# Pooled rows kept whole in HBM and split where they are fetched, in a hybrid encoder block on one Trainium2 core

## The chip, the cores and the metric

One core of one Trainium2 chip runs the whole kernel. The metric is the device time of one execution in microseconds (us). A core has five engines with a queue of instructions each: TensorE (PE, matrix products), VectorE (DVE), ScalarE (ACT), GpSimd (POOL) and SyncE (SP, which here only issues transfers). An engine works its queue in order: an instruction that waits holds everything behind it on the same engine. Transfers (DMAs) are issued here from SP's and from ACT's queue.

## The reference

One layer (`DEPTH = 1`) of a bidirectional hybrid encoder on x (1 x 1024 x 1024, float32):

```python
h = rmsnorm(x, norm_mix)
q, k, v, r, lr_f, lr_b, u, g_a, g_b = split(h @ w_in)
y_a = swish-gated, normed gated linear attention, forward plus backward, @ w_branch_gla
y_b = per group: (multiscale_pool(u)[g] @ w_pool_group[g]) * pool_scale
x = x + (sigmoid(g_a) * y_a + sigmoid(g_b) * y_b) @ w_out
x = x + swiglu(rmsnorm(x, norm_ffn) @ w_ffn_in) @ w_ffn_out
```

and a final RMSNorm. What matters here is branch B. `u` has 512 channels in four groups of 128; for group g, `multiscale_pool` takes a centred mean over 2, 4, 8 or 16 positions (only valid ones at the ends) and subtracts the token itself:

```python
window_sum = cs[:, hi, gi] - cs[:, lo, gi]
return window_sum / count - ug
```

Each pooled group (128 channels x 1024 positions) is then multiplied by a 128 x 256 matrix and by the gate `sigmoid(g_b)`.

## The kernel before

**Arithmetic.** Every matrix product is made in full precision from reduced-precision parts (`fp32r`). An operand is split into a high part, cast by ACT, and a low part, the difference, made by DVE or POOL; three matmuls (hi x hi, lo x hi, hi x lo) are added up in PSUM (`products`, L288-L291, so nearly all matmuls have the line L291). The large projections go through a seven-product scheme: of two 2 x 2 blocked operands, seven products of sums of blocks are formed in place of eight. One product of this kind is 12 matmuls of 128x512.

**Stages.** Norm and projections of q, k, v; the two scans of the attention; then the *gate stage* (L1316-L1361); then the branch products, the merge with `w_out`, the feed-forward layer and the last norm. The gate stage makes the columns of `w_in` for the pool input and the gates in ten units of 256 columns, n = 0 to 9: units 0 and 1 are the pool input `u`, 2 to 5 gate A, 6 to 9 gate B. Run n of the loop over `gate_runs` has seven products, in the order 1, 5, (product 4 of unit n-1), 6, 2, 3, 7; the last run also does its own product 4 at the end. `at` counts the products in a run. In `Gates.run`, the results of products 1, 6 and 5 are copied by ACT to the row `ga` (L1281), those of 2, 3 and 7 added to it by DVE (L1286), and a sigmoid follows on ACT (L1289). Banks of PSUM are shared: 1, 6, 7 and 4 of a unit accumulate in one, 5 and 3 in another, so product 6 waits until the copy of product 1 is done, product 7 for the copy of 6, product 3 for that of 5, and product 4 for the add of 7. For a gate-B unit g = n - 6, after products 7 and 4, `Gates.pooling` makes the group's own product `yb` from the split pooled rows `ph`, `pl` and the split `w_pool_group` (three blocks after 7, one after 4).

**Weights.** A unit's weight halves are loaded by SP (`fraw`, L910), summed by DVE where the scheme wants a sum (`fs`, L918), cast by ACT (`wh`, L198) and their low parts made mostly by POOL (`wl`, L199).

**What sets the order.** After every three matmuls `mm3` calls `pump` with the share of a product's quarter that has passed (1 for 512 columns). `pump` runs what is due: steps put off with `soon(delay, step)`, stores that were put on a list with `later` (`pending`), one generator of jobs (`aside`) and one generator of side work (`side`). Each of these yields a cost, and the next step comes when as many units of `pump` have passed. So the numbers in the source set at which place in each engine's queue a step is written, and nothing is reordered later.

**Pooling** is the generator `pooling` (L1235), begun in run 2 at `at == 4`. For each group it loads the rows of `u`, calls `pooled` (window sums on DVE in tiles `ws`, per half of the 1024 positions), and stores the result to `p_out` in HBM. `pooled` yields after each operation and `pooling` multiplies this cost by `POOLING`. `load_pooled(g)` brings it back into two slots (`ph`, `pl`) in run 6 + g.

**Feed-forward jobs.** Two units of `w_ffn_in` (`READY = 2`) get their seven weight operands in the gate stage: `unit_jobs` loads two raw halves into slots (`fraw`, L534), POOL makes four sums in place (L637), and each of the seven operands is cast by ACT (`uph`, L629), gets its low part from DVE (`upl`, L620), and both parts are stored to HBM in `u_out` from ACT's queue (L631, L616). The parts stand in the pool `t2`, which has five buffers that pooling's `u` and `ws` also use. The jobs come through `prepare_beside(jobs, 2.7, ...)`, one step each 2.7 units of `pump`.

## Time and profile before

| What | us |
|---|---|
| three runs | 1383.60, 1383.58, 1387.52 (median 1383.6) |
| the profiled execution | 1385.57 |
| its span, first to last instruction | 1383.8 |
| PE busy | 1362.2 (98%) |
| DVE, POOL, ACT busy | 848.3, 757.6, 625.1 |
| mean granted TensorE clock | 0.999 of full speed |

Times in the traces count from the start of the span. In a row of a timeline stand the start in us, the duration in us, the engine, the line of the kernel, the operation, output and inputs by the program's names, the shape, and in brackets how long the engine was idle ahead of it and what ended that. In a table of waits stand the engine, its waiting operation, what it waited for, then us in total, how often and the longest. In a tile's view stand the durations min/median/max in ns and the first and last start in us.

### The profile page before, as it was taken

What the parts mean: (1) busy time and instruction counts of PE and PEld (TensorE: products, weight loads), DVE (VectorE), ACT (ScalarE), POOL (GpSimd) and SP (SyncE); (2) the same over time, 40 slices, a digit from 0 to 9 for tenths busy, and PEclk for the clock granted to TensorE, in tenths of its full rate; (3) what the DMA queues carried; (4) which work ended last, traced back from release to release, by engine and by line L of the source; (5) the groups of instructions that cost most, each with busy time, mean ns of one, the idle gap of its engine ahead of it and who ended that gap; (6) DMA issues with size and microseconds to landing.
All of it is one profiled execution on the core that took longest, in us unless ns stands there. A gap on an engine that the chain in (4) does not pass through costs nothing.

```text
span 1383.8 us, 18503 instructions
## 1 busy us (share of the span) xinstructions
PE 1362.2 (98%) x6654; PEld 1150.9 (83%) x6654; DVE 848.3 (61%) x1073; ACT 625.1 (45%) x1125; POOL 757.6 (55%) x565
## 2 busy tenths in 40 slices
PE   7999999999999999999999999999999999999997
PEld 7889898988888877788888788888888888888886
DVE  6276767766645885587884856555655556343374
ACT  7365655644334444554346533333333334453252
POOL 3260715312398456568665276666666667464354
PEclk9999999999999999999999999999999999999999
DMA  6221322321487669997416355555444447975451
GB/s 193 77 92 44 110 82 87 122 77 46 138 264 238 211 198 310 334 393 257 152 61 240 118 175 175 175 175 175 159 141 141 145 137 267 385 256 216 167 232 73
DMA packets 167452, 243.56 MB, mean 176 GB/s; under 512 B 10904, under 2 KB 97856, under 8 KB 167360
## 3 DMA queue, kind: packets, MB, share of 16 engines
q1 hardware_dynamic: 154368, 215.11, 46.7%
q10 hardware_dynamic: 12992, 27.27, 5.3%
q8 instruction: 52, 0.85, 0.3%
q14 instruction: 40, 0.33, 0.1%
HBM read 164.48 MB, written 77.86 MB: 175 GB/s over the span
## 4 chain that ended last, share of the span: by engine, by line
PE 81%; POOL 5%; issue 4%; DVE 4%; ACT 3%; DMA 2%; ACTq 0%; POOLq 0%; SPq 0%; DVEq 0%
PE ps L291 75%; POOL wl L199 2%; PE op L849 2%; DMA u_out<-uph 1%; PE kv L291 1%; PE sc L777 1%; PE op L291 1%; POOL qe L733 1%; DVE res L1796 1%; POOL wsum L637 1%; PE yb L291 1%; PE tp L1008 1%; DMA u_out<-upl 0%; DMA raw<-in_w_in_dram 0%; DVE ws L1068 0%
## 5 line engine op out<-in xcount | busy, mean ns | idle before, releaser
L199 POOL TENSOR_TENSOR wl<-fs,wh 128x512 fp32r<-128x512 f32 x120 | 166.2, 1389 | 163.9 <-ACT wh L198 139.4
L291 PE MATMUL ps<-gl,wh 128*128 128x512 f32 x616 | 239.8, 389 | 0.9 <-DVE gl L1488 0.9
L291 PE MATMUL ps<-gh,wh 128*128 128x512 f32 x616 | 240.4, 390 | 0.0
L291 PE MATMUL ps<-gh,wl 128*128 128x512 f32 x616 | 239.7, 389 | 0.0
L199 POOL TENSOR_TENSOR wl<-fraw,wh 128x512 fp32r<-128x512 f32 x90 | 130.1, 1445 | 64.3 <-ACT wh L198 59.5
L199 POOL TENSOR_TENSOR wl<-raw,wh 128x512 fp32r<-128x512 f32 x44 | 63.8, 1463 | 159.0 <-ACT wh L198 158.9
L199 POOL TENSOR_TENSOR ol<-gor,oh 128x1024 fp32r<-128x1024 f32 (+1 forms) x42 | 99.8, 2382 | 92.3 <-ACT oh L198 71.8
L291 PE MATMUL ps<-hh,wh 128*128 128x512 f32 x376 | 149.8, 398 | 0.0
L291 PE MATMUL ps<-hh,wl 128*128 128x512 f32 x376 | 146.6, 390 | 0.0
L291 PE MATMUL ps<-hl,wh 128*128 128x512 f32 x376 | 146.5, 390 | 0.0
L291 PEld LDWEIGHTS ps<-gl,wh 128*128 128x128 f32 x616 | 115.7, 188 | 25.1 <-DVE gl L1488 1.3
L291 PEld LDWEIGHTS ps<-gh,wl 128*128 128x128 f32 x616 | 115.6, 188 | 24.0
L291 PEld LDWEIGHTS ps<-gh,wh 128*128 128x128 f32 x616 | 115.7, 188 | 23.6
L291 PE MATMUL ps<-ol,oh 128*128 128x512 f32 x308 | 119.9, 389 | 0.2 <-DVE ol L199 0.2
L291 PE MATMUL ps<-oh,oh 128*128 128x512 f32 x308 | 119.8, 389 | 0.0
L291 PE MATMUL ps<-oh,ol 128*128 128x512 f32 x308 | 119.8, 389 | 0.0
L199 POOL TENSOR_TENSOR wl<-wraw,wh 128x512 fp32r<-128x512 f32 x56 | 91.3, 1659 | 46.0 <-ACT wh L198 46.0
L199 DVE TENSOR_TENSOR ol<-wor,oh 128x1024 fp32r<-128x1024 f32 (+1 forms) x41 | 61.4, 1520 | 49.5 <-ACT oh L198 49.3
L198 ACT CAST wh<-fs 128x512 fp32r<-128x512 f32 x120 | 73.8, 615 | 32.1 <-DVE fs L918 23.8
L291 PEld LDWEIGHTS ps<-hh,wl 128*128 128x128 f32 x376 | 70.6, 188 | 15.0
L291 PEld LDWEIGHTS ps<-hl,wh 128*128 128x128 f32 x376 | 70.7, 188 | 13.2
L291 PEld LDWEIGHTS ps<-hh,wh 128*128 128x128 f32 x376 | 70.7, 188 | 13.2
(262 smaller groups left out, 3176.4 us busy)
## 6 DMA issues: line engine op xcount, KB each, us to landing
fraw<-in_w_ffn_in_dram SPq DMA_DIRECT2D x44, 512.0 KB, 6.2
gor<-g_out SPq DMA_DIRECT2D x35, 512.0 KB, 7.1
raw<-in_w_in_dram SPq DMA_DIRECT2D x48, 256.0 KB, 3.8
g_out<-s SPq DMA_DIRECT2D x44, 256.0 KB, 2.3
fraw<-in_w_in_dram SPq DMA_DIRECT2D x20, 512.0 KB, 4.5
wor<-t_out SPq DMA_DIRECT2D x20, 512.0 KB, 7.6
g_out<-g SPq DMA_DIRECT2D x33, 256.0 KB, 2.6
x<-in_x_dram SPq DMA_DIRECT2D x16, 512.0 KB, 4.3
```

Source lines behind the costliest of these rows:

```text
L198: nc.scalar.copy(hi, src)
L199: eng.tensor_tensor(lo, src, as_f32(hi), op=ALU.subtract)
L291: nc.tensor.matmul(ps, a[i], b[j], start=first and n == 0, stop=last and n == 2, skip_group_check=onto)
L637: op()
L733: nc.gpsimd.tensor_tensor(e_q[:, d, :], e_q[:, d, :], q[:, half, :], op=ALU.mult)
L777: nc.tensor.matmul(sc[d][:, i * CH : (i + 1) * CH], chunk_of(ke, n, d), chunk_of(qe, n, d), start=True, stop=True,)
L849: nc.tensor.matmul(op[:, :DV], a, b, start=False, stop=j == len(terms) - 1)
L1008: nc.tensor.transpose(tp[:, i * P : (i + 1) * P], o_heads[j // 2][half][:, i, (j % 2) * P : (j % 2 + 1) * P], ident[:, :],)
L1796: nc.vector.scalar_tensor_tensor(res[:, COLS[j]], x2[t][:, COLS[j]], rs[:, :], gain_final[:, COLS[j]], op0=ALU.mult, op1=ALU.mult)
```

## The change

`pooled` no longer splits its result. The last operation of each half writes straight into one tile of 128 x 2 x 512 float32, and the group is stored with one transfer of 512 KB. `load_pooled` fetches it with one transfer into the slot `pl`, one product earlier than before (`at == 2` for 3). Two new steps split it on the spot: `cast_pooled` takes a second slot `ph` and casts all 1024 columns on ACT; `low_pooled` subtracts in place on DVE. They are put off by 2.5 and 4.3 units from the end of `at == 4` (in the last run of `at == 3`). `POOLING` goes from 1.75 to 2.5 and two yields around the stores go. And the two feed-forward units are begun at `at == 1` of run 6 where it was `at == 4`, three products sooner.

```diff
-POOLING = 1.75
+POOLING = 2.5
...
-    def pooled(g, u, hi, lo):
+    def pooled(g, u, raw):
...
             nc.vector.scalar_tensor_tensor(
-                s[:, body], s[:, body], 1.0 / width, u[half][:, body], op0=ALU.mult, op1=ALU.subtract
+                raw[:, half, :], s[:, body], 1.0 / width, u[half][:, body], op0=ALU.mult, op1=ALU.subtract
             )
             yield 1
-            nc.scalar.copy(hi[:, half, :], s[:, body])
-            yield 1
-            nc.vector.tensor_tensor(lo[:, half, :], s[:, body], as_f32(hi[:, half, :]), op=ALU.subtract)
-            yield 0.2
...
-    p_out = dram.tile([GROUPS, 2, P, 2, HALF], F32, name="p_out")
+    p_out = dram.tile([GROUPS, P, 2, HALF], F32, name="p_out")
...
-        pools[g] = [slot(F32R, s=s) for s in ("ph", "pl")]
-        for n, t in enumerate(pools[g]):
-            nc.sync.dma_start(as_f32(t[:, :, :]), p_out[g][n])
+        t = slot(F32R, s="pl")
+        nc.sync.dma_start(as_f32(t[:, :, :]), p_out[g])
+        pools[g] = [None, t]
+
+    def cast_pooled(g):
+        pools[g][0] = slot(F32R, s="ph")
+        nc.scalar.copy(pools[g][0][:, :, :], as_f32(pools[g][1][:, :, :]))
+
+    def low_pooled(g):
+        hi, t = (t[:, :, :] for t in pools[g])
+        nc.vector.tensor_tensor(t, as_f32(t), as_f32(hi), op=ALU.subtract)
...
-            hi, lo = slot(F32R, s="ph"), slot(F32R, s="pl")
-            for cost in pooled(g, u, hi, lo):
+            raw = slot(s="pr")
+            for cost in pooled(g, u, raw):
                 yield POOLING * cost
-            nc.scalar.dma_start(p_out[g][0], as_f32(hi[:, :, :]))
-            yield 4
-            nc.scalar.dma_start(p_out[g][1], as_f32(lo[:, :, :]))
+            nc.scalar.dma_start(p_out[g], raw[:, :, :])
             stored.add(g)
-            yield 1
+            yield 2
...
                 if n == 2:
                     begin(pooling(), 4)
-                if n == 6:
-                    finish_side()
-                    finish_beside()
-                    prepare_beside(map(unit_jobs, range(READY)), 2.7, 1, 1, nc.scalar)
+            if n == 6 and at == 1:
+                finish_side()
+                finish_beside()
+                prepare_beside(map(unit_jobs, range(READY)), 2.7, 1, 1, nc.scalar)
...
-            if n >= 6 and at == (0 if last else 3):
+            if n >= 6 and at == (0 if last else 2):
                 load_pooled(n - 6)
+            if n >= 6 and at == (3 if last else 4):
+                soon(2.5, partial(cast_pooled, n - 6))
+                soon(4.3, partial(low_pooled, n - 6))
```

PE's instructions stand in the same order in both kernels. The changed kernel's lines lie a few numbers lower or higher: L1281, L1286 and L1289 become L1283, L1288 and L1291.

*DVE, end of unit 5 (run 5).* `ga` is the row of unit 5's results (the adds of product 3 and of product 7), `ws` and `u` are pooling's window sums and rows of group 3. Before:

```order
L1286 TENSOR_TENSOR ga_4978<-ps_4984,ga_4978 128x512
L1088 TENSOR_TENSOR pl_5049<-ws_5089,ph_5048 128x512
L1068 TENSOR_TENSOR ws_5118<-u_5024 128x527
L1074 TENSOR_TENSOR ws_5126<-ws_5118 128x525
L1286 TENSOR_TENSOR ga_5000<-ps_4961,ga_5000 128x512
```

Now:

```order
L1288 TENSOR_TENSOR ga_4970<-ps_4976,ga_4970 128x512
L1074 TENSOR_TENSOR ws_5098<-ws_5079 128x521
L1074 TENSOR_TENSOR ws_5106<-ws_5098 128x513
L1288 TENSOR_TENSOR ga_4992<-ps_4950,ga_4992 128x512
```

Between the two adds the low part and the first two sums of the second half are gone, and the two last sums of that half have come.

*SP, run 7.* The transfers for group 1 of the pooled rows, for the next gate unit (`fraw`, L910) and for the second feed-forward unit (`fraw`, L534). Before:

```order
L910 DMA fraw_5354<-in_w_in_dram 128x8x128
L910 DMA fraw_5384<-in_w_in_dram 128x8x128
L1223 DMA ph_5422<-p_out 128x1024
L1223 DMA pl_5423<-p_out 128x1024
L534 DMA fraw_5481<-in_w_ffn_in_dram 128x8x128
L534 DMA fraw_5482<-in_w_ffn_in_dram 128x8x128
L1227 DMA wpr_5493<-in_w_pool_group_dram 128x256
```

Now:

```order
L910 DMA fraw_5357<-in_w_in_dram 128x8x128
L534 DMA fraw_5389<-in_w_ffn_in_dram 128x8x128
L534 DMA fraw_5390<-in_w_ffn_in_dram 128x8x128
L910 DMA fraw_5399<-in_w_in_dram 128x8x128
L1218 DMA pl_5405<-p_out 128x1024
L1231 DMA wpr_5473<-in_w_pool_group_dram 128x256
```

The two feed-forward loads stand ahead of the gate unit's second half and of the pooled rows, where they stood behind both.

*ACT, run 7.* `uph`, `u_out` belong to the feed-forward jobs, `wh` are the casts of the next gate unit's weights. Before:

```order
L629 CAST uph_5441<-fraw_5267 128x512
L631 DMA u_out_7_666<-uph_5441 128x512
L1289 ACTIVATE ga_5329<-ga_5329 128x512
L500 DMA yb_out<-ga_5153 256x1x512
L500 DMA yb_out<-ga_5175 256x1x512
L198 CAST wh_5456<-fs_5430 128x512
L616 DMA u_out_5_664<-upl_5416 128x512
L629 CAST uph_5467<-fraw_5266 128x512
```

Now:

```order
L616 DMA u_out_3_662<-upl_5394 128x512
L1291 ACTIVATE ga_5322<-ga_5322 128x512
L500 DMA yb_out<-ga_5135 256x1x512
L500 DMA yb_out<-ga_5154 256x1x512
L198 CAST wh_5451<-fs_5431 128x512
L1223 CAST ph_5466<-pl_5405 128x1024
L1291 ACTIVATE ga_5322<-ga_5322 128x512
L198 CAST wh_5475<-fs_5455 128x512
L629 CAST uph_5492<-fraw_5390 128x512
```

The last job of the first feed-forward unit is issued ahead of the sigmoid where two of its seven casts were still to come, and the cast of the pooled rows stands between two weight casts; the low part's subtraction follows on DVE behind the add of product 3.

## The prediction, made before the change was timed

> **What bounds the kernel now.** I read the page's busy times first, then the waits of PE, then the gate stage (run 0 to run 9, some 390 to 590 us) in windows, then each PE gap there in the timeline. The page's first part:

> ```profile
> PE 1362.2 (98%) x6654; PEld 1150.9 (83%) x6654; DVE 848.3 (61%) x1073; ACT 625.1 (45%) x1125; POOL 757.6 (55%) x565
> ```

> PE is busy for 1362.2 of 1383.8 us. The change leaves every PE instruction in its place, so it can only move PE's gaps. These are PE's waits over the span (us in total, times, longest):

> ```profile
> PE vps L451 <- DMA rows<-in_norm_mix_dram: 5.2, 1, 5.2
> PE tr L338 <- DVE xn L327: 2.6, 2, 2.2
> PE ps L291 <- ACT ga L1281: 1.6, 1, 1.6
> PE ps L291 <- DVE ga L1286: 1.4, 2, 0.8
> PE ps L291 <- DVE gl L1488: 0.9, 1, 0.9
> ...
> PE ps L291 <- DVE dl L163: 0.7, 1, 0.7
> ```

> The first two are the kernel's start; `gl` and `dl` come after the gates. The gate stage has only the three waits on `ga`, 1.6 + 1.4 us. In PE's timeline they stand here, each row behind the matmul before it:

> ```profile
> 496.65 0.39 PE L291 MATMUL ps<-trh,wl 128*128 128x512 f32 x1
> 497.87 0.50 PE L291 MATMUL ps<-trh,wh 128*128 128x512 f32 x1 [0.83 <-DVE ga L1286]
> ...
> 540.82 0.39 PE L291 MATMUL ps<-trh,wl 128*128 128x512 f32 x1
> 541.74 0.50 PE L291 MATMUL ps<-trh,wh 128*128 128x512 f32 x1 [0.54 <-DVE ga L1286]
> ...
> 553.24 0.39 PE L291 MATMUL ps<-hh,wl 128*128 128x512 f32 x1
> 555.24 0.50 PE L291 MATMUL ps<-trh,wh 128*128 128x512 f32 x1 [1.61 <-ACT ga L1281]
> ```

> Matmuls that wait for nothing follow each other by 0.23 us (the rows 533.49 and 533.72 below). So the three steps of 1.22, 0.92 and 2.00 us lose 0.99, 0.69 and 1.77: **3.45 us**, 0.25% of 1383.6. That is all this region can give. About 0.3% (4.15 us) is what a measurement of this kernel tells from no change.

> **Why they wait.** First gap, DVE; second, DVE; third, ACT:

> ```profile
> 493.38 1.38 DVE L1088 TENSOR_TENSOR pl<-ws,ph 128x512 fp32r<-128x512 f32 x1 [0.81 <-ACT ph L1086]
> 494.68 1.79 DVE L1068 TENSOR_TENSOR ws<-u 128x527 f32<-128x527 f32 x1
> 496.51 0.71 DVE L1074 TENSOR_TENSOR ws<-ws 128x525 f32<-128x525 f32 x1
> 497.13 0.68 DVE L1286 TENSOR_TENSOR ga<-ps,ga 128x512 f32<-128x512 f32 x1
> ```

> ```profile
> 540.16 0.93 DVE L620 TENSOR_TENSOR upl<-fraw,uph 128x512 fp32r<-128x512 f32 x1 [3.79 <-DMA u_out<-upl]
> ```

> ```profile
> 553.58 0.62 ACT L629 CAST uph<-fraw 128x512 fp32r<-128x512 f32 x1 [4.82 <-DMA u_out<-uph]
> 554.60 0.59 ACT L1281 COPY ga<-ps 128x512 f32<-128x512 f32 x1 [0.40 <-ACT uph L629]
> ```

> The add at 497.13, for which product 7's bank waits, stands behind three pooling operations, the first of which waited 0.81 us for ACT. The second and third stand behind feed-forward jobs that wait 3.79 and 4.82 us for a buffer whose store has not landed.

> **The change, part by part.** The splits of the pooled rows, before, and the nearest rows for the whole-row split that replaces them (a cast and an fp32r subtraction of 128x1024 elsewhere in the program):

> ```profile
> L1086 ACT CAST ph<-ws x8: 615/621/624, 439.7 to 502.7; 128x512 fp32r<-128x512 f32 x8
> L1088 DVE TENSOR_TENSOR pl<-ws,ph x8: 693/1019/1375, 440.3 to 503.4; 128x512 fp32r<-128x512 f32 x8
> ...
> L1129 ACT CAST dh<-ob x12: 1037/1050/1056, 576.8 to 645.7; 128x1024 fp32r<-128x1024 f32 x12
> ...
> L163 DVE TENSOR_TENSOR dl<-ob,dh x12: 1210/1353/2318, 577.9 to 647.7; 128x1024 fp32r<-128x1024 f32 x12
> ```

> Removed: on ACT 8 x 0.62 = 5.0 us, on DVE 8 x 1.02 = 8.2, four stores and four loads of 512 KB (4 MB). Added, later: on ACT 4 x 1.05 = 4.2, on DVE 4 x 1.35 = 5.4 (1.21 to 2.32 each). By itself that is worth nothing: both engines have slack. What counts is where it stands.

> First gap: DVE's order now has two `ws` sums (0.7 each) between product 3's and product 7's adds, where before a low, a 527 sum and a 525 sum stood (1.38 + 1.79 + 0.71, and 0.81 of waiting). That frees 0.81 + 3.88 - 1.42 = 3.3 us, more than the 0.99 lost. I take **-0.99**; bounds 0 and -0.99, since a gap can only be closed. The wider pace (`POOLING` 2.5) pays nothing back: on ACT the last pooled store now stands before the first product of run 6 begins to copy, ahead of where `finish_side` would force it.

> Second and third gaps: the jobs of both units start three products sooner. Windows (us, then busy us of PE, PEld, DVE, ACT, POOL, the granted clock, DMA share, GB/s):

> ```profile
> 490.00:510.00 20.00, 19.17 (x85) 15.54 (x84) 17.78 (x21) 9.80 (x19) 10.24 (x7) 1.00 0.62 202
> 510.00:530.00 20.00, 20.00 (x89) 16.47 (x88) 11.53 (x16) 9.33 (x18) 11.54 (x9) 1.00 0.93 276
> 530.00:550.00 20.00, 19.46 (x86) 15.72 (x85) 10.33 (x14) 10.48 (x19) 13.45 (x10) 1.00 0.93 292
> ```

> The DMA engines are at 0.62 until 510 and 0.93 after; the earlier jobs begin in the lighter part, and 4 MB less is moved. In the new order product 7's add of run 7 (the second gap) stands ahead of unit 1's first job on DVE, where before unit 0's last one came first. Product 6's copy of run 8 (the third) stands behind unit 1's last cast on ACT, where before it stood behind the fourth, but jobs that run 6.5 us sooner leave it time (worked out below for run 7). I take both gaps as closed, **-0.69 - 1.77 = -2.46**; bounds 0 (the wait for buffers only moves along) and -2.46.

> Now what is given back. SP's order puts the pooled load of run 7 last: after two feed-forward loads and the second half of the gate weight. It takes the buffer of unit 0's raw weight, so it waits for the fifth job's low on DVE and for POOL's third `L637` sum; behind it come `cast_pooled` on ACT, `low_pooled` on DVE and then PE's `yb`. The rows for that chain are ACT's, then POOL's, DVE's sum of two weight halves (min/median/max ns), and PE's `yb` of group 0 and the first of group 1:

> ```profile
> 510.67 0.60 ACT L198 CAST wh<-fs 128x512 fp32r<-128x512 f32 x1
> ...
> 517.66 0.62 ACT L629 CAST uph<-fraw 128x512 fp32r<-128x512 f32 x1
> ...
> 531.97 1.21 ACTq L500 DMA_DIRECT2D yb_out<-ga  x2
> ```

> ```profile
> 517.84 1.29 POOL L199 TENSOR_TENSOR wl<-fs,wh 128x512 fp32r<-128x512 f32 x1 [2.78 <-ACT wh L198]
> ...
> 525.15 1.74 POOL L637 TENSOR_TENSOR fraw<-fraw 128x512 f32<-128x512 f32 x1
> 526.98 1.63 POOL L637 TENSOR_TENSOR fraw<-fraw,fraw 128x512 f32<-128x512 f32 x1
> ```

> ```profile
> L918 DVE TENSOR_TENSOR fs<-fraw x8: 686/1342/1779, 402.2 to 552.3; 128x512 f32<-128x512 f32 x8
> ```

> ```profile
> 522.36 0.40 PE L291 MATMUL yb<-ph,wpl 128*128 128x512 f32 x1
> ...
> 533.49 0.40 PE L291 MATMUL yb<-ph,wph 128*128 128x512 f32 x1
> 533.72 0.39 PE L291 MATMUL yb<-pl,wph 128*128 128x512 f32 x1
> ```

> From a DMA's issue to its landing (min, median, max us), for loads of `pl`, for `fraw` and for the jobs' stores `u_out` between 400 and 600 us:

> ```profile
> DMA to landing us min/median/max: 6.2/7.8/9.5
> ```

> ```profile
> DMA to landing us min/median/max: 3.8/5.5/7.9
> ```

> ```profile
> DMA to landing us min/median/max: 2.8/4.7/9.1
> ```

> Unit 0's first cast moves from 517.66 to behind the cast at 510.67, some 6.5 us. The fifth job's low needs the store of the second job's low, which is issued behind the weight cast that feeds the POOL row 517.84, so at about 517.8, and lands at 522.5; with 0.93 for the low, 523.4. POOL's way is shorter: its second and third sums come behind 517.84, 517.84 + 1.29 + 1.63 + 1.74 = 522.5. The `yb` at 522.36 frees the buffers of the two loads ahead at 522.8. So the pooled load goes out at 523.4 and lands at 531.2; cast 1.05 and low 1.35 give 533.6, where PE wants `pl` at 533.72. Margin 0.1 us at medians: the fastest of each gives 2.5 us to spare (522.8 + 6.2 + 1.04 + 1.21 = 531.3), the slowest store 9.1 with a median load 4.3 us of wait, with the slowest load 6.0. A second way ends in the same place: the second half weight, issued 522.8, lands 528.3, and its sum (L918) stands ahead of product 2's add on DVE; with 1.34 for the sum and 0.68 for the add, ACT goes on at 530.3, issues two `yb_out` (1.21), casts a weight (0.62), then `ph` (1.05), then the low (1.35): 534.5, a wait of 0.8. I take **+1.5** for run 7, bounds 0 and 6.0, near the medians. Run 8's load is bound in the same way to unit 1's jobs, with no load of a feed-forward weight ahead: **+0.9**, bounds 0 and 6.0. Runs 6 and 9 wait for no job, but split two steps before use: **+0.1** each, bounds 0 and 1 (the low at its slowest, 2.32 for 1.35). Everything shifts by the 0.99 of the first gap together, since these chains hang on PE's copies.

> Behind the last jobs of a unit stand, on ACT, the seventh product's weight cast and product 6's copy. POOL's fourth sum ends at 522.5 + 1.29 + 1.74 = 525.5, the last job's cast, a small one and the weight's take it to 527, the weight's low (1.29) to 528.3; the seventh product needs both 12 matmuls ahead of 533.49, at 530.8. Zero, with 2.5 us of cover; a store landing at 9.1 instead of 4.7 would use it up and cost 1.9.

> Sum: -3.45 + 1.5 + 0.9 + 0.2 = **-0.85**. The profiled execution took 1385.57 us, of which 1383.8 is the span; it would become 1384.7. It is 1.97 above the median of 1383.6, so the median goes to **1382.7**.

> **The rivals.** *All three gaps go and nothing comes back:* 1383.6 - 3.45 = 1380.1. For it: 2.5 us to spare with quick landings. Against it: the 0.93 of the windows.

> *The wait for buffers moves along with the jobs* (the change doesn't do what it says): only the first gap goes, and the pooled loads cost 2.6: 1383.6 - 0.99 + 2.6 = 1385.2. For it: jobs of one unit need five buffers' stores landed whenever they run. Against it: 0.62 in the windows where they now begin.

> *The order on SP's queue.* Three loads of 512 KB go out within about 0.6 us, the pooled one last. At 276 to 292 GB/s the 1.5 MB take 5.4 to 5.7 us if nothing else moves, and 11 us if the stores from ACT take half. Landing at 534.4 for 531.2 and 2.4 more makes a wait of 3.1 in run 7: 1383.6 - 3.45 + 3.1 + 1.1 = 1384.3. For it: `pl`'s landings (7.8) are longer than `fraw`'s (5.5), and it was the later of a pair; against it: none was over 9.5. [...]

> *Slower: the fifth job holds the pooled load.* Place: the `yb` of runs 7 and 8. If stores land after 9.1 instead of 4.7 us in both, each waits 4.3: 1383.6 - 3.45 + 8.6 + 0.2 = 1388.9. It decides from a store landing of about 8.5 on (a wait of 3.7 each turns -3.45 into +4.15 with the 0.2). For it: the row at 553.58, held 4.82 us by just such a store; against it: these stores now begin earlier, and 9.1 is the longest of that row.

> **How the numbers follow.** The forecast 0.42, all gained 0.20, moved along 0.15, SP's queue 0.10, slower 0.13. Only the second can reach 1379.45, and only with luck beyond its sum; slower needs 1387.75, which the last nearly always passes and the third and fourth rarely: faster 0.06, same 0.80, slower 0.14. The range 1379.8 to 1387.0 holds all but the last and a little at the low end.

> **What would show it.** After: no wait `ps <- ga` over 0.3 us in the gate stage (gaps 1 to 3); DVE's `pl` lows of 128x1024 at 1.2 to 2.3 us; a wait of PE's `yb` on the DVE low, of 0 to 3 us in runs 7 and 8; the pooled load of run 7 issued within 1 us of 523. Wrong if `ga` waits stay, if `yb` waits over 4 us, or if PE waits for a weight's low from POOL in these runs.

## The result

The changed kernel takes 1392.57 us (median of 6 runs, 1390.62 to 1393.99) where the kernel before takes 1385.6 on the same chips: ratio **1.0055**, interval 1.0044 to 1.0065. It is slower by 7 us, outside the range forecast, and on the side that had 0.14. The profiled execution is 1393.99 us with a span of 1392.3, 8.5 longer than before's span.

PE's waits over the span of the changed kernel (us in total, times, longest), the largest four:

```profile
PE yb L291 <- ACT ph L1223: 5.6, 2, 4.6
PE vps L451 <- DMA rows<-in_norm_mix_dram: 5.1, 1, 5.1
PE tr L338 <- DVE xn L327: 2.8, 2, 2.3
PE yb L291 <- DVE pl L1227: 1.7, 2, 1.0
```

No row `ps <- ga` is left: the three gaps of the kernel before are closed. In their place `yb` waits four times, twice for the cast of the pooled rows and twice for their low part. Here is run 7 in PE's timeline:

```profile
532.70 0.39 PE L291 MATMUL ps<-trh,wl 128*128 128x512 f32 x1
537.67 0.80 PE L291 MATMUL yb<-ph,wph 128*128 128x512 f32 x1 [4.58 <-ACT ph L1223]
539.15 0.80 PE L291 MATMUL yb<-pl,wph 128*128 128x512 f32 x1 [0.69 <-DVE pl L1227]
539.74 0.63 PE L291 MATMUL yb<-ph,wpl 128*128 128x512 f32 x1
540.17 0.63 PE L291 MATMUL yb<-ph,wph 128*128 128x512 f32 x1
...
542.61 0.39 PE L291 MATMUL ps<-hh,wh 128*128 128x512 f32 x1
542.84 0.39 PE L291 MATMUL ps<-hl,wh 128*128 128x512 f32 x1
```

And run 8:

```profile
562.17 0.39 PE L291 MATMUL ps<-trh,wl 128*128 128x512 f32 x1
563.56 0.51 PE L291 MATMUL yb<-ph,wph 128*128 128x512 f32 x1 [1.01 <-ACT ph L1223]
565.05 0.50 PE L291 MATMUL yb<-pl,wph 128*128 128x512 f32 x1 [0.98 <-DVE pl L1227]
565.38 0.40 PE L291 MATMUL yb<-ph,wpl 128*128 128x512 f32 x1
```

Against the free step of 0.23 us the steps of 4.97, 1.48, 1.39 and 1.49 lose 4.74 + 1.25 + 1.16 + 1.26 = **8.4 us**. There is a second loss that no wait shows: from 539.74 on, matmuls that wait for nothing follow each other by 0.43 us instead of 0.23. The windows give the granted clock, the third number from the right:

```profile
520.00:540.00 20.00, 14.73 (x61) 11.53 (x60) 10.96 (x14) 9.42 (x17) 10.43 (x7) 0.89 0.78 264
540.00:560.00 20.00, 20.00 (x84) 16.37 (x84) 14.60 (x17) 9.22 (x18) 13.35 (x10) 0.94 0.80 265
560.00:580.00 20.00, 18.01 (x72) 14.12 (x71) 8.32 (x11) 7.83 (x14) 8.29 (x7) 0.91 0.82 287
```

It was 1.00 in all of these before. The steps above 0.3 us add up to 1.64 us behind run 7's wait and 1.67 behind run 8's: **3.3 us**. With the 3.45 us of the closed gaps (and 0.3 of slightly longer steps behind them) that makes 8.4 + 3.3 - 3.8 = 7.9 of the 8.5 us.

What held run 7's cast can be followed upward. The chain of waits names a transfer first:

```profile
523.39 10.06 DMA fraw<-in_w_in_dram
```

It ends in DVE's sum of the two weight halves, behind which the add of product 2 stands; ACT's sigmoid waits for the add, two issues of `yb_out` and a weight cast stand behind the sigmoid, and only then comes the cast of the pooled rows:

```profile
533.47 0.69 DVE L918 TENSOR_TENSOR fs<-fraw 128x512 f32<-128x512 f32 x1 [4.71 <-DMA fraw<-in_w_in_dram]
534.08 0.68 DVE L1288 TENSOR_TENSOR ga<-ps,ga 128x512 f32<-128x512 f32 x1
```

```profile
534.79 0.63 ACT L1291 ACTIVATE ga<-ga 128x512 f32<-128x512 f32 x1 [6.24 <-DVE ga L1288]
534.80 1.21 ACTq L500 DMA_DIRECT2D yb_out<-ga  x2
536.05 0.62 ACT L198 CAST wh<-fs 128x512 fp32r<-128x512 f32 x1 [0.63 <-issue]
536.58 1.04 ACT L1223 CAST ph<-pl 128x1024 fp32r<-128x1024 f32 x1
```

The cast at 536.58 itself waits for nothing: the pooled rows were there, though not long before. Their packets, the only ones of 4096 bytes on SP's queue there, end at 534.1. The transfer that DVE waited for stood on SP behind the two feed-forward loads, and its issue, begun at 523.39, took 2.03 us:

```profile
522.18 1.11 SPq L534 DMA_DIRECT2D fraw<-in_w_ffn_in_dram  x2
523.39 2.03 SPq L910 DMA_DIRECT2D fraw<-in_w_in_dram  x1
525.52 2.08 SPq L1218 DMA_DIRECT2D pl<-p_out  x1
```

### The profile page after: what moved, and what is told of

Read it like the earlier page. It is cut to its first block, busy times and chain, and to the rows that moved or that the text cites. A ratio compares the mean times of both kernels' runs of the same rounds, so it can differ in the third digit from the quotient of the medians.

```text
span 1392.3 us, 18482 instructions
## 1 busy us (share of the span) xinstructions
PE 1366.1 (98%) x6654; PEld 1153.7 (83%) x6654; DVE 845.5 (61%) x1069; ACT 626.0 (45%) x1121; POOL 757.9 (54%) x565
## 4 chain that ended last, share of the span: by engine, by line
PE 87%; DVE 3%; POOL 3%; issue 3%; ACT 2%; DMA 1%; ACTq 0%; SPq 0%; POOLq 0%; DVEq 0%
PE ps L291 80%; PE op L849 2%; POOL wl L199 1%; PE kv L291 1%; PE yb L291 1%; PE sc L777 1%; PE op L291 1%; DMA fraw<-in_w_in_dram 1%; DVE res L1801 1%; POOL wsum L637 1%; POOL qe L733 1%; PE tp L1008 1%; PE tr L338 1%; DMA x<-in_x_dram 0%; POOL mg L1195 0%
## 5 line engine op out<-in xcount | busy, mean ns | idle before, releaser
L199 POOL TENSOR_TENSOR wl<-fs,wh 128x512 fp32r<-128x512 f32 x120 | 165.2, 1380 | 177.1 <-ACT wh L198 147.6
L291 PE MATMUL ps<-gl,wh 128*128 128x512 f32 x616 | 239.8, 389 | 0.9 <-DVE gl L1493 0.9
L291 PE MATMUL ps<-gh,wh 128*128 128x512 f32 x616 | 240.4, 390 | 0.0
L291 PE MATMUL ps<-gh,wl 128*128 128x512 f32 x616 | 239.7, 389 | 0.0
L199 POOL TENSOR_TENSOR wl<-fraw,wh 128x512 fp32r<-128x512 f32 x90 | 128.5, 1428 | 59.8 <-ACT wh L198 59.2
L199 POOL TENSOR_TENSOR wl<-raw,wh 128x512 fp32r<-128x512 f32 x44 | 63.7, 1462 | 159.1 <-ACT wh L198 156.0
L291 PE MATMUL ps<-hh,wh 128*128 128x512 f32 x376 | 150.2, 400 | 0.0
L199 POOL TENSOR_TENSOR ol<-gor,oh 128x1024 fp32r<-128x1024 f32 (+1 forms) x42 | 99.0, 2365 | 92.5 <-ACT oh L198 79.1
L291 PE MATMUL ps<-hl,wh 128*128 128x512 f32 x376 | 147.0, 391 | 0.0
L291 PE MATMUL ps<-hh,wl 128*128 128x512 f32 x376 | 146.9, 391 | 0.0
L291 PEld LDWEIGHTS ps<-gl,wh 128*128 128x128 f32 x616 | 115.6, 188 | 25.1 <-DVE gl L1493 1.3
L291 PEld LDWEIGHTS ps<-gh,wl 128*128 128x128 f32 x616 | 115.6, 188 | 24.1
L291 PEld LDWEIGHTS ps<-gh,wh 128*128 128x128 f32 x616 | 115.6, 188 | 23.6
L291 PE MATMUL ps<-ol,oh 128*128 128x512 f32 x308 | 119.9, 389 | 0.2 <-DVE ol L199 0.2
L291 PE MATMUL ps<-oh,ol 128*128 128x512 f32 x308 | 119.8, 389 | 0.0
L291 PE MATMUL ps<-oh,oh 128*128 128x512 f32 x308 | 119.8, 389 | 0.0
L199 POOL TENSOR_TENSOR wl<-wraw,wh 128x512 fp32r<-128x512 f32 x56 | 94.6, 1718 | 44.1 <-ACT wh L198 44.0
L199 DVE TENSOR_TENSOR ol<-wor,oh 128x1024 fp32r<-128x1024 f32 (+1 forms) x41 | 60.9, 1507 | 49.5 <-ACT oh L198 45.8
L198 ACT CAST wh<-fs 128x512 fp32r<-128x512 f32 x120 | 73.8, 615 | 30.7 <-DVE fs L918 25.4
L291 PEld LDWEIGHTS ps<-hh,wl 128*128 128x128 f32 x376 | 70.9, 188 | 15.1
L291 PEld LDWEIGHTS ps<-hh,wh 128*128 128x128 f32 x376 | 71.1, 189 | 13.5
L291 PEld LDWEIGHTS ps<-hl,wh 128*128 128x128 f32 x376 | 71.0, 189 | 13.3
```

Source lines behind the costliest of these rows:

```text
L198: nc.scalar.copy(hi, src)
L199: eng.tensor_tensor(lo, src, as_f32(hi), op=ALU.subtract)
L291: nc.tensor.matmul(ps, a[i], b[j], start=first and n == 0, stop=last and n == 2, skip_group_check=onto)
```

## The experiments

All ratios are against the kernel before, timed on the same chip in the same round. Two theories stood at the start. **A:** the next gate unit's second weight half, queued behind the feed-forward loads, is late and holds DVE, and so ACT. **B:** fetching raw and splitting in two serial steps so late is slow by itself. **C** is the forecast's own slower rival and the price it gave to SP's order: the pooled load decides.

**The change without the earlier start.**

```diff
-            if n == 6 and at == 1:
+            if n == 6 and at == 4:
                 finish_side()
```

> The change with the two feed-forward units begun where they were before (at == 4 of run 6); pooled rows whole, pace and on-the-spot split as in the change. Theory A (the next gate unit's second weight half is queued behind the feed-forward loads, lands 10 us after its issue, and holds DVE's adds and with them ACT's cast of ph): the half weight is ahead of those loads again, so yb waits under 1 us in runs 7 and 8, the waits of the feed-forward jobs on ga (0.7 and 1.8 us) come back, 1383 to 1386 us. Theory B (fetching the rows raw and splitting them in two serial steps is late by itself): yb waits 3 us or more in run 7 and over 2 in run 8, and the matmuls after it run slower as in the change, 1390 us or more.

Measured 1391.04 us, ratio 1.0045 (1.0031 to 1.0059). With the half weight ahead of the feed-forward loads `yb` still waits, 2.5 us in run 7 and 3.4 in run 8, close to theory B. Waits of PE between 380 and 640 us:

```profile
PE yb L291 <- ACT ph L1223: 3.4, 2, 2.3
PE yb L291 <- DVE pl L1227: 2.5, 2, 1.4
```

In this kernel the cast of run 8 stands behind other late things on ACT: a job's cast that waited 2.90 us for POOL's sum, then the sigmoid, two `yb_out` issues that took 2.29 us, a weight cast and another job. So A alone is not the cause. The gaps on `ga` did not come back; PE's own waits at `yb` ahead of them would explain that.

**The earlier start alone,** on the kernel before:

```diff
-                if n == 6:
-                    finish_side()
-                    finish_beside()
-                    prepare_beside(map(unit_jobs, range(READY)), 2.7, 1, 1, nc.scalar)
+            if n == 6 and at == 1:
+                finish_side()
+                finish_beside()
+                prepare_beside(map(unit_jobs, range(READY)), 2.7, 1, 1, nc.scalar)
```

> The kernel before with nothing changed but the start of the two feed-forward units (at == 1 of run 6). Theory A: SP's order in run 7 is that of the change (half weight, then both pooled parts, behind the two feed-forward loads), so DVE's sum of the weight halves waits 3 to 5 us there; no cast of ph stands behind it, but the pooled parts come last on the queue, so yb waits 1 to 5 us for its DMA: 1386 to 1391 us. Theory B: no wait of yb, the two ga waits behind feed-forward jobs gone, 1381 to 1384 us.

Measured 1386.92 us, ratio 1.0016 (1.0007 to 1.0025): slower by about 2 us, the low end of theory A. DVE's sum waits only 1.01 us for the half weight where 3 to 5 were expected. PE's waits between 380 and 640 us:

```profile
PE yb L291 <- DMA pl<-p_out: 1.8, 2, 1.0
PE ps L291 <- ACT ga L1281: 1.0, 2, 0.5
PE ps L291 <- DVE ga L1286: 0.7, 1, 0.7
PE ps L291 <- POOL wl L199: 0.5, 1, 0.5
```

`yb` waits for the pooled load, which SP now issues last; two small waits on ACT's copies stand where a larger one was. The gap near 497 us is still there (0.88 us). So the earlier start does not pay with the pooled loads where they are.

**The second unit later,** so that run 7's half weight and pooled load are ahead of its two feed-forward loads:

```diff
-                prepare_beside(map(unit_jobs, range(READY)), 2.7, 1, 1, nc.scalar)
+                prepare_beside(map(unit_jobs, range(1)), 2.7, 1, 1, nc.scalar)
+            if n == 7 and at == 3:
+                finish_beside()
+                prepare_beside(map(unit_jobs, range(1, READY)), 2.7, 1, 1, nc.scalar)
```

> The change, but the second feed-forward unit is begun only at at == 3 of run 7, so that SP issues run 7's second half weight and pooled rows ahead of its two loads. Theory A: the half weight lands 4 to 6 us after its issue, yb waits under 1 us in run 7, run 8 as in e1 or better, 1382 to 1386 us. Theory B: yb waits as in the change (4.6 + 0.7 in run 7), 1390 us or more.

Measured 1390.37 us, ratio 1.0036 (1.0023 to 1.0049). The half weight, issued at 522.48 with the pooled load and the two feed-forward loads right behind it, lands in 5.1 us:

```profile
DMA to landing us min/median/max: 5.1/5.1/5.1
```

Run 7's wait for the cast falls from 4.58 to 0.23 us, as A says; the wait for the low (1.00) stays, and run 8 now waits 3.14 for its cast, which the jobs of the second unit hold up on ACT. Neither theory has the whole.

**The pooled load first,** at the run's first product:

```diff
-            if n >= 6 and at == (0 if last else 2):
+            if n >= 6 and at == 0:
                 load_pooled(n - 6)
```

> The change with the pooled rows loaded at at == 0 of their run, first on SP's queue and ahead of the feed-forward loads; the half weight stays behind them, the split stays where it is. Theory A: the rows are there early but DVE's sum still waits for the half weight until about 533 us, ACT reaches the cast of ph as late as in the change, yb waits 3 to 5 us in run 7: 1389 to 1393 us. Theory C (the pooled load itself, held by the fifth job and last on the queue, sets the wait): the wait goes, 1382 to 1386 us.

Measured 1393.48 us, ratio 1.0062 (1.005 to 1.0075). The load of run 7 goes out at 508.92, 14 us sooner than the half weight, and `yb` waits longer than in the change:

```profile
533.85 0.69 DVE L918 TENSOR_TENSOR fs<-fraw 128x512 f32<-128x512 f32 x1 [5.92 <-DMA fraw<-in_w_in_dram]
```

```profile
538.06 0.80 PE L291 MATMUL yb<-ph,wph 128*128 128x512 f32 x1 [5.79 <-ACT ph L1223]
```

That refutes C: the pooled load is issued 28 us ahead of the cast (536.96), and the cast is as late as in the change, held by the half weight through DVE and ACT.

The four together gave **theory D**: what costs is the *place* of the split. It stands on ACT behind a sigmoid that waits for DVE, behind two `yb_out` issues and behind jobs, about 2 us ahead of PE's use; whatever is late on either engine then reaches PE, in run 7 the half weight, in run 8 the jobs.

**Early load, early split, second unit later.** The two edits just shown, and

```diff
-            if n >= 6 and at == (3 if last else 4):
-                soon(2.5, partial(cast_pooled, n - 6))
-                soon(4.3, partial(low_pooled, n - 6))
+            if n >= 6 and at == 3:
+                soon(2.5 if last else 0.5, partial(cast_pooled, n - 6))
+                soon(4.3 if last else 2.0, partial(low_pooled, n - 6))
```

> The change with the second feed-forward unit later (as in e3), the pooled rows loaded at at == 0 (as in e4), and the split moved about two products ahead (cast and low 0.5 and 2.0 after at == 3): the cast stands ahead of the sigmoid and the two yb_out issues on ACT, the low ahead of product 2's add on DVE. Theory D (what costs is the place of the split: it stands on ACT behind yb_out's issues and whatever is late there, some 2 us before PE wants it): no wait of yb, no slow matmuls, 1380 to 1384 us. If raw fetching costs in another way, yb still waits over 1 us and the time is over 1386.

Measured **1381.3 us**, ratio 0.9981 (0.9972 to 0.999), faster than both kernels. PE has no wait left in the gate stage and the clock stays at full speed. Run 7 on ACT, DVE and PE:

```profile
528.47 1.05 ACT L1223 CAST ph<-pl 128x1024 fp32r<-128x1024 f32 x1
532.69 0.64 ACT L1291 ACTIVATE ga<-ga 128x512 f32<-128x512 f32 x1 [3.18 <-DVE ga L1288]
532.70 1.21 ACTq L500 DMA_DIRECT2D yb_out<-ga  x2
```

```profile
530.23 0.69 DVE L918 TENSOR_TENSOR fs<-fraw 128x512 f32<-128x512 f32 x1 [2.02 <-DMA fraw<-in_w_in_dram]
530.84 1.22 DVE L1227 TENSOR_TENSOR pl<-pl,ph 128x1024 fp32r<-128x1024 f32 x1
```

```profile
532.40 0.40 PE L291 MATMUL yb<-ph,wph 128*128 128x512 f32 x1
532.64 0.39 PE L291 MATMUL yb<-pl,wph 128*128 128x512 f32 x1
```

The cast now stands ahead of the sigmoid and ends some 3 us early. The sigmoid still waits 3.18 us for DVE, and that costs PE nothing. The low ends at 532.06, 0.6 us ahead of its use, since it still stands behind the half weight's sum.

**The same early split with both feed-forward units in the order of the change** (only the second unit's start put back):

> The change with the pooled rows loaded at at == 0 and the same early split, but both feed-forward units in their order as in the change. Theories A and D together: run 7's low stands behind the sum of the late half weight on DVE, which ends at about 534, so yb waits 2 to 3 us there and a weight for run 8 is late by 1 to 2; run 8 has no wait: 1385 to 1389 us. Theory D alone (the late half weight is harmless once the cast is early): 1381 to 1384.

Measured 1388.05 us, ratio 1.0031 (1.0019 to 1.0043). Run 7's `yb` takes the cast at once and then waits for the low, which stands on DVE behind the sum that the late half weight holds:

```profile
533.43 0.69 DVE L918 TENSOR_TENSOR fs<-fraw 128x512 f32<-128x512 f32 x1 [6.02 <-DMA fraw<-in_w_in_dram]
534.04 1.22 DVE L1227 TENSOR_TENSOR pl<-pl,ph 128x1024 fp32r<-128x1024 f32 x1
```

```profile
531.61 0.40 PE L291 MATMUL yb<-ph,wph 128*128 128x512 f32 x1
535.32 0.52 PE L291 MATMUL yb<-pl,wph 128*128 128x512 f32 x1 [3.31 <-DVE pl L1227]
```

So A and D are both needed. The wait expected on a weight of run 8 was instead one of 1.26 on ACT's copy (`ga`).

**The same early split with both units begun where they were before** (`at == 4` of run 6):

> The same early load and split with the feed-forward units begun where they were before: pooled rows whole and the wider pace alone. Theory D: no wait of yb, the waits of ga behind feed-forward jobs (0.7 and 1.8 us in the kernel before) come back in part: 1381 to 1385 us. Otherwise yb waits as in e1, 1389 or more.

Measured 1388.34 us, ratio 1.0029 (1.0017 to 1.0042), which was not expected. `yb` waits for nothing, as D says; but the gaps behind the jobs come back larger than before:

```profile
PE ps L291 <- DVE ga L1288: 4.5, 3, 2.5
PE ps L291 <- ACT ga L1283: 1.3, 1, 1.3
```

The longest stands behind a job's low that waited 3.91 us for a store. The stores `u_out` took a median of 6.6 us to land here, 4.7 in the kernel before and 3.8 in the best version. Why they took that long was not settled; the pair shows only that the best version's starts of the two units avoid these gaps.

**The wider pace alone,** on the kernel before (`POOLING = 2.5`):

> The kernel before with the wider pace alone (POOLING 2.5). Pooling of group 3 is then not done when it is drained in run 6, and its second half stands in one piece on DVE ahead of run 6's add of product 3. If the pace was what closed the gap at 497.87, that gap goes but run 6 waits 3 us or more for the add: 1386 to 1390 us. If the removed splits closed it, the gap stays and so does the time: 1384 to 1386.

Measured 1384.38 us, ratio 1.0002 (0.9993 to 1.0011): no change that can be told. In its profile the gap near 497 us is gone, and the wait of 3 us that was expected for the drained pooling is not there; one gap of 1.07 us on ACT's copy is left in the stage.

**The old split with the new starts and the pace:** the kernel before with `POOLING = 2.5`, the first feed-forward unit at `at == 1` of run 6 and the second at `at == 3` of run 7.

> The kernel before with its pooled rows split ahead of the store, the wider pace, the first feed-forward unit begun at at == 1 of run 6 and the second at at == 3 of run 7. If the gain of the best version so far comes from the starts of the feed-forward units and the pace, and the whole rows only need to do no harm, this gives the same: no wait in the gate stage over 1 us, 1380 to 1383 us. If the whole rows carry it (fewer transfers and less work on ACT and DVE), waits of 2 us or more in sum remain: 1383 to 1386 us.

Measured 1387.28 us, ratio 1.002 (1.0012 to 1.0029), above what either case gave. The last group is stored late (its low part is issued at 505.62), so run 6's copy and both pooled loads come late:

```profile
PE ps L291 <- ACT ga L1281: 1.3, 1, 1.3
PE yb L291 <- DMA ph<-p_out: 1.0, 1, 1.0
PE yb L291 <- DMA pl<-p_out: 0.8, 1, 0.8
```

So with the old split the best version's gain is not had at this pace. All the loss stands in run 6, though: from 519 to 640 us PE has no wait, so the new starts close the second and third gap with the old split too. The old split with the new starts at the old pace was not run; how much of the gain needs the whole rows stays open.

**The best version at the old pace** (`POOLING = 1.75`):

> The version with the early load, the early split and the second unit later, at the old pace (POOLING 1.75). If the pace alone closed the gap at 497.87, that gap (1 us) is back and the time is 1 us above that version, 1382 to 1383 us; if the removed splits are enough, it is the same, 1380.5 to 1382.

Measured 1382.47 us, ratio 0.9975 (0.9966 to 0.9984), the same as at the wider pace within the intervals (0.9972 to 0.999), and no wait of PE in the gate stage. The gap near 497 us closes by either edit, the pace or the removed splits.

**The best version with the split back in the change's place:**

> That version with the split back at the place it has in the change (2.5 and 4.3 after at == 4), early load and later second unit kept. Theory D (the place of the split): yb waits in run 8 as in e3, 3 to 4.5 us, and slow matmuls after it, 1388 to 1391 us. If the load was what mattered, no wait: 1381 to 1383 us.

Measured 1390.02 us, ratio 1.004 (1.0026 to 1.0054), and PE's waits in the stage are those of the third experiment again:

```profile
PE yb L291 <- ACT ph L1223: 3.5, 2, 3.1
PE yb L291 <- DVE pl L1227: 1.7, 2, 1.0
```

The pooled load of run 8 goes out at 534.93 and the cast starts only at 557.67, behind a job's cast that waited 2.78 us for POOL, the sigmoid, two issues of `yb_out` (1.22), a weight cast and a store's issue. Between this kernel and the best one only the place of the split differs: 0.6% of the time.

## Why the prediction was wrong

**The gaps: right.** The terms -0.99 and -2.46 came as priced: no wait on `ga` is left in the changed kernel. That alone would not show the reason given for the second and third, since they also vanish in the first experiment, without the earlier start. The best version shows it: no `yb` waits there, and the gaps are closed; with the old starts (the seventh experiment) they are back.

**The step that failed: the term of run 7, +1.5 for 6.0 measured.** Its place was right, in "the second way". The prediction followed the second half weight through DVE's sum, product 2's add, the sigmoid, two `yb_out` and a weight cast to the split, and gave it a wait of 0.8 us (the term of the sum, +1.5, covers this way and the pooled load's), where run 7 lost 6.0, because it took the half weight as issued at 522.8 and landing 5.5 us later, the median row of the kernel before. In the trace SP reached it at 523.39, its issue took 2.03 us (0.38 for that gate unit's first half at 513.11), and DVE had it at 533.47: 10.1 us from 523.39. From there on the sum was right within 0.8 us: 533.47 to the cast's end at 537.62 is 4.2 us, and the prediction had 528.3 to 533.2, 4.9. A median of landings from another order of the queue was used for a transfer that now had two others of 512 KB ahead of it. Run 7 is 4.5 us of the 9.3 between the forecast of -0.85 and the 8.5 of the spans; run 8 is 1.5 and the clock 3.3.

**The rival on SP's queue** had that mechanism, but for the pooled rows, and at a chance of 0.10. For it the 5.4 to 11 us of landing are borne out (10.1), on the half weight. Experiment three issues the same four loads within 2 us in the other order, and the half weight lands in 5.1 us instead of 10.1. The place in the queue is not all: in the best version, with one load ahead of it, the half weight issued at 522.02 reached DVE at 530.23, 8.2 us later. The rival was also right about the pooled rows: it had them landing at 534.4, and their last packet ended at 534.1. What they alone would have cost, with the half weight on time, was not run.

**The slower rival** named the place, `yb` of runs 7 and 8, and a price (8.6 us of waits) close to the 8.4 measured, but through the fifth job that would hold the pooled load. The fourth experiment rules that out: with the load 16.6 us earlier (508.92 for 525.52) `yb` waits 5.79 us. So the price was right by luck. The sign named beforehand, a pooled load issued within 1 us of 523, failed too: SP came to it at 525.52, behind the issue of the half weight.

**The low's term.** The cast and the low were summed as a chain of 1.05 + 1.35 and the slack set against the second matmul of `yb`. That was right, and it is why each late split costs PE twice: the first matmul waits for the cast, the second 1.25 us more for the low (1.45 us on DVE, in both runs).

**Run 8** was given +0.9; it lost 1.16 + 1.26. The reason written down (jobs hold the load) was not it: the load, issued at 552.04, landed 6.5 us later, 3.9 us ahead of the cast at 562.47, and in the fourth experiment, with the load out at 538.36, the same two steps lose 1.53 + 1.26. The cast stood behind the sigmoid and issues of 2.07 us. For run 8 nothing that stands ahead of the split on ACT was priced.

**The clock** was not in the sum: 3.3 us, 40% as much again as the waits ahead of it.

## What to carry to other kernels

When work is moved behind a fetch, look at what stands ahead of it on each engine's queue at its new place, and not only at how long it takes: the same split written about two products earlier turned +0.4% into -0.2%. A landing time measured at one place in a queue need not hold at another: the half weight took 10.1 us with two loads of its size ahead of it (the change), 8.2 with one (the best version) and 5.1 with the same two behind it (the third experiment). A chain with a margin of 0.1 us at medians is a likely loss, since the wait adds up and the gain does not.

## What the runs showed of the hardware that was not expected

Behind some of PE's waits the matmuls ran at 0.43 us a step instead of 0.23, though they waited for nothing; the granted clock was 0.50 there. Here are the places in the gate stage where such steps followed or PE lost over 2.5 us in one stretch. The idle time is that of the steps over the free one, added where only a matmul or two lie between. The last column is explained below.

| Kernel | PE idle, us | slow matmuls, us lost | PE busy in the piece ahead, us |
|---|---|---|---|
| the change without the earlier start, run 7 | 1.22 + 1.71 | 8, 1.63 | 1.04 |
| the change without the earlier start, run 8 | 2.47 + 1.30 | 8, 1.66 | 0.50 |
| the change, run 7 | 4.74 + 1.25 | 8, 1.64 | 0.88, 0.80 |
| the change, run 8 | 1.16 + 1.26 | 9, 1.67 | 1.80 |
| pooled load first, run 7 | 5.95 + 1.24 | 14, 2.96 | 0.20, 0.80, 2.77 |
| pooled load first, run 8 | 1.53 + 1.26 | none | 2.01 |
| second unit later, run 8 | 3.30 + 1.03 | 9, 1.65 | 0.89 |
| early split, units as in the change, run 7 | 3.48 | 9, 1.68 | 0.34 |
| early split, units as before, run 8 | 2.62 | none | 1.98 |
| old split, new starts, run 6 | 1.14 + 1.05 | 9, 1.65 | 1.65 |
| split back in the change's place, run 8 | 3.22 + 1.02 | 7, 1.44 | 0.49 |

In the changed kernel the clock is 0.50 from 535.62 to 542.45 and from 566.34 to 569.75, for twice 3.41 us and for 3.41. The length of the wait ahead does not tell whether one follows: 2.19 us in two parts were enough once (1.14 + 1.05) and 2.79 another time were not (1.53 + 1.26). What fits all these places is how much of the wait falls into one piece of a fixed grid. Cut a trace into pieces of 3.41 us from the edge of one of its slow stretches; the other slow stretches then begin and end at cuts (in the changed kernel the two begin 30.72 us apart, nine pieces, and the first of them 153 pieces after the clock's first rise at 13.38). The last column gives PE's busy time in the piece ahead of each slow one (without a slow one, in the piece where PE was least busy). Here are two such pieces in run 8 of the change and two in run 8 of the pooled load first; the first number behind the comma is PE's busy time, the third from the right the clock:

```profile
562.93:566.34 3.41, 1.80 (x7) 1.25 (x8) 2.80 (x3) 2.33 (x5) 2.51 (x2) 1.00 0.67 258
566.34:569.75 3.41, 3.41 (x10) 2.65 (x9) 2.93 (x5) 0.43 (x1) 1.28 (x1) 0.50 0.87 293
...
562.78:566.19 3.41, 2.01 (x8) 1.12 (x6) 1.73 (x3) 2.78 (x5) 1.28 (x1) 1.00 0.76 293
566.19:569.60 3.41, 2.45 (x11) 2.00 (x12) 3.41 (x5) 1.60 (x3) 2.17 (x2) 1.00 0.75 257
```
